# Strassen's scheme for eight more blocks of the first up projection and two more of the second, with the S5 setup batched over all groups

## The chip, the cores and the metric

The kernel runs on one core of a Trainium2 chip. The metric is the time of one execution in microseconds on the device; the time before is the median of three runs. One more execution was recorded by the hardware profiler.

## The reference

One decoder layer on a sequence of 512 tokens with 1024 channels, in float32:

```python
mod = (silu(c) @ w_ada + b_ada).reshape(9, 1024)      # sh1 sc1 g1 sh2 sc2 g2 sh3 sc3 g3
h = x * (1 + sc1) + sh1
x = layer_norm(ALPHA * x + 0.5 * g1 * ((silu(h @ w1) * (h @ w3)) @ w2))      # ffn1, 2816 wide
h = x * (1 + sc2) + sh2
x = layer_norm(ALPHA * x + g2 * hybrid_mixer(h))      # a Mamba-2 head group and an S5 head group
h = x * (1 + sc3) + sh3
x = layer_norm(ALPHA * x + 0.5 * g3 * ((silu(h @ w1) * (h @ w3)) @ w2))      # ffn2
```

The S5 group has 32 groups of 64 complex states. Before its scan can run, powers of the states' factors, and products of them with the input matrix B (called P) and the output matrix C (called Q), must be made from the parameters: this is the S5 setup.

## The kernel before

Every float32 matrix product is made of three matmuls: each operand is split into a high part (a rounded copy, made by ScalarE in `split`) and a low part (the rest, a subtraction on VectorE), and `mm3` adds high x high, high x low and low x high in PSUM (lines 101 to 105, so each product shows as L103, L104 and L105).

The up projections make 22 blocks f of 128 hidden channels, each with two matrices j (w1 and w3). In a plain block one such product has 8 steps of the inner dimension, 128x128 weights and 512 tokens: 24 matmuls of 512 columns. Of the second up projection the first two blocks are done in halves of the tokens, blocks 2 to 5 plainly, and blocks 6 to 21 (`FAST = 6`) in pairs by Strassen's scheme in `up_fast`: one unit is a pair of blocks and one j, a 2 x 2 arrangement of quarters (two halves of the inner dimension, two halves of the tokens, two blocks), with seven products (b11, t1, t2, b21, b22, t3, t4) of 4 steps with 256 columns, 84 matmuls. Sums of the weights (`wsum`, and sums written back into the raw tiles) are made for each unit by VectorE in `prep_a`, `prep_c`; sums of the activations once, by `h_sums`, into the three tiles `hs`, with a last one (`s4`) written over a quarter of the activations after the plain blocks.

Of the first up projection the first three blocks and half of the fourth run with the adaLN of h1 at the very start (to 60 us); the rest (`up`, line 1537) are plain blocks. Beside them run two lists of generators, advanced a fixed number of steps in each block: `jobs` holds the S5 setup (4 steps a block) and `ada`, from block 11 on, the remaining adaLN work (3 steps a block): loads of x, `ada_gate` for chunk 2 (g1), `ada_pair` for chunks 3 and 4 (m2), `ada_pair` for 6 and 7 (m3), `ada_gate` for chunk 5 (g2). One chunk is eight loads of 512 KB (tile `ra`, two buffers) each multiplied into one accumulator `acc` by VectorE (operations on L90), and then matmuls with ones (L295 for pairs, L318 and L319 for gates). What is left of `ada` is advanced once for each f of the first down projection (38 calls), and the rest is emptied behind it.

The S5 setup first computes parameters in 128x16 tiles, then runs four rounds b, each for four of the 16 pairs of groups: P, Q (128x64 operations), the matrices that are written to DRAM through the tile `s5mp` (two buffers, five uses a round), and the powers E (`Er`, `Ei`), which double their width seven times.

The down projections go over f in pairs, with `ghl` the split hidden activations, and end with a drain for each 128 tokens: the residual, the LayerNorm statistics, the normalisation and (first down) the transposed activations `hT` of the next stage.

The program is written in one order, and the framework's planner orders the instructions of each engine from it, so an instruction can stand earlier on its engine than it is written. Weights go over one queue, SP's, in a fixed order through four `raw` tiles; `wnext` splits two tiles ahead. `gate` rows have two buffers, and `wsum` takes one of them in the second up projection.

Of the kernel before, what the change touches and what calls it, by code (L numbers as in the profile page):

```python
# [10 lines left out]
F32 = mybir.dt.float32  # L11
# [8 lines left out]
P = 128  # L20
S = 512
# [29 lines left out]
class Layer:  # L51
    def __init__(self, tc, ctx, ins, out):
        self.tc, self.nc, self.ctx = tc, tc.nc, ctx
        self.i = ins
        self.out = out
        self.n = 0
        pool = lambda name, bufs, **k: ctx.enter_context(tc.tile_pool(name=name, bufs=bufs, **k))
        self.cp = pool("const", 1)
        self.ps = pool("ps", 8, space=PSUM)
        self.raw = pool("raw", 4)  # L60
        self.wsp = pool("wsp", 4)
        self.resp = pool("res", 1)
# [7 lines left out]
        self.pin = False  # L70

# [311 lines left out]

    def glue(self, gp, g, f, pa, pb):
        nc = self.nc
        if f % 2 == 0:
            self.gt = gp.tile([P, 2, S], F32, tag="g", bufs=NF // 2, name=self.nm("g"))
# [51 lines left out]
    def h_sums(self, hq, new, gp, gts):  # L439

        nc = self.nc
        v = lambda k, t: hq[k][:, 2 * t:2 * t + 2]
        hi, lo = lambda a: a[:, :, :, 0, :], lambda a: a[:, :, :, 1, :]
        for _ in range(3):
            gts.append(gp.tile([P, 2, S], F32, tag="g", bufs=NF // 2, name=self.nm("g")))
# [24 lines left out]
        join(y, v(1, 0))  # L472
        yield
        self.stt(y, y, -1.0, x, MUL, SUB)
        self.s4 = lambda: split(y, v(0, 1))

    def up_fast(self, hq, new, gp, gts, g, w, f0, last, jobs):
# [5 lines left out]
        v = lambda k, t: hq[k][:, 2 * t:2 * t + 2]  # L483
# [23 lines left out]
        c = self.gates.tile([P, 1024], F32, tag="gate", bufs=2, name="wsum")  # L507
# [45 lines left out]
        for u, (f, j) in enumerate(units):  # L553
            if j == 0:
                gt = gts.pop() if gts else gp.tile([P, 2, S], F32, tag="g", bufs=NF // 2, name=self.nm("g"))
                g.extend((gt[:, 0, :], gt[:, 1, :]))
            cp = self.tmp.tile([P, 4, 256], F32, tag="t4", name=self.nm("cp"))
# [19 lines left out]
            self.step(jobs, 1)  # L577
# [197 lines left out]
    def s5_setup(self, pre):  # L775
# [61 lines left out]
        E = (pt("Er", [P, 4, P]), pt("Ei", [P, 4, P]))  # L837
        w3 = [P, 4, 16]
        Pk = [(pt(f"p{k}r", w3), pt(f"p{k}i", w3)) for k in range(4)]
        Qk = [(pt(f"q{k}r", w3), pt(f"q{k}i", w3)) for k in range(4)]  # L840
        u1, u2 = pt("s5u1", w3), pt("s5u2", w3)
        mpart = lambda: pre.tile([P, 4, P], F32, tag="s5mp", bufs=2, name=self.nm("s5mp"))
        for b in range(4):
            q = slice(4 * b, 4 * b + 4)
            wb = lambda a: bc(a[:, q], (2, 16))
            dr = self.s5_dram[b]
            self.cmul(*Pk[0], wb(fr), wb(fi), bt['s5_b_re'][:, q], bt['s5_b_im'][:, q], u1, u2)
            for k in (1, 2, 3):
                if k == 2:
                    yield  # L850
                self.cmul(*Pk[k], wb(A[k][0]), wb(A[k][1]), *Pk[0], u1, u2)
            yield
            for n in range(2):
                for g in range(2):
                    sl = slice(64 * g, 64 * g + 64)
                    for k in range(4):
                        nc.scalar.copy(out=bd[n][sl, :, 3 - k, g, :], in_=Pk[k][n][sl])
                    nc.scalar.mul(out=cd[n][sl, :, g, :], in_=cb[('s5_c_re', 's5_c_im')[n]][sl, q, :],
                                  mul=(1.0, -1.0)[n])
            yield  # L860
            for j in range(4):
                if j == 2:
                    yield
                self.cmul(*Qk[j], wb(A[j + 1][0]), wb(A[j + 1][1]), cb['s5_c_re'][:, q],
                          cb['s5_c_im'][:, q], u1, u2)
# [9 lines left out]
            for n in range(2):  # L875
                M = mpart()
                nc.gpsimd.memset(M, 0.0)
                for g in range(2):
                    sl = slice(64 * g, 64 * g + 64)
                    for j in range(4):  # L880
                        nc.scalar.mul(out=M[sl].rearrange("p r (j g h) -> p r j g h", j=4, g=2)[:, :, j, g, :],
                                      in_=Qk[j][n][sl], mul=(1.0, -1.0)[n])
                nc.sync.dma_start(out=dr[:, 5 + n], in_=M)
                yield
            nc.vector.memset(E[0][:, :, 0:1], 1.0)
            nc.vector.memset(E[1][:, :, 0:1], 0.0)
            x1, x2 = [pre.tile([P, 4, 64], F32, tag="s5x", bufs=2, name=self.nm("s5x")) for _ in range(2)]
            for lg in range(7):
                n = 1 << lg
                er, ei = en[lg]  # L890
                self.cmul(E[0][:, :, n:2 * n], E[1][:, :, n:2 * n], bc(er[:, q], (2, n)), bc(ei[:, q], (2, n)),
                          E[0][:, :, 0:n], E[1][:, :, 0:n], x1[:, :, :n], x2[:, :, :n])
                if lg % 2 == 1:
                    yield
            for n in range(2):
                nc.sync.dma_start(out=dr[:, 2 + n], in_=E[n])
            yield
# [533 lines left out]
def body(tc, ins, out):  # L1431
# [3 lines left out]
    with ExitStack() as ctx:  # L1435
# [7 lines left out]
        L.want_up(ins['up1'], EARLY)  # L1443
        TAIL = 4
        HALVES = 2
        FAST = 6
# [12 lines left out]
        L.want_down(NF, ins['ffn1_w2'][0])  # L1459
        L.wlimit = len(L.wq)  # L1460
        L.want_mixer()
        L.want_up(ins['up2'], (), HALVES, g_alloc, FAST)
# [136 lines left out]
        gts = []  # L1599
        jobs = [L.h_sums(hx, hs, fp, gts), L.ada_gate(8, 0.5, g3)]  # L1600
        fast = L.up_fast(hx, hs, fp, gts, g, ins['up2'], FAST, down2, jobs)
        lead = [(next(fast) for _ in range(4))]
        L.up(hT3[0], fp, g, 0, jobs, 4, halves=HALVES, late=(lead, 4, FAST - 1), nf=FAST)
# [45 lines left out]
```

## Time and profile before

| | |
|---|---|
| median of three runs | 966.59 us (966.46 to 968.69) |
| profiled execution: its own time | 968.27 us |
| its span (first to last instruction) | 966.6 us |
| TensorE (PE) busy | 944.9 us, 98% |
| VectorE (DVE) busy | 758.4 us, 78% |
| ScalarE (ACT) busy | 446.9 us, 46% |
| GpSimd (POOL) busy | 34.2 us, 4% |
| mean granted TensorE clock | 0.995 |

The span is what the trace covers; 1.67 us of the profiled execution lie around it. Busy times are unions: an operation that starts before the last one has ended adds only what stands out. PE is the matmul row, PEld the weight loads beside it. The stages lie so: first up projection to 269.5 us, first down projection to 391, the mixer to 615, the second up projection to 838 (Strassen's units from 675), the second down projection to the end.

### The profile page before, as it was taken

How to read it: one execution, taken by the hardware profiler on the slowest of the kernel's cores; microseconds unless marked ns; L12 is line 12 of the kernel's file. 1: busy time of each engine (PE TensorE's matmuls, PEld its weight loads, DVE VectorE, ACT ScalarE, POOL GpSimd, SP SyncE). 2: the span in 40 equal slices, each digit the busy share in tenths (PEclk: the TensorE clock that was granted, in tenths of full speed). 3: DMA queues.
4: the chain of work that ended last, by engine and by line, in shares of the span. 5: the costliest groups of instructions: out<-in, count | busy, mean ns of one | idle time of the engine just before them, and what ended most of it. 6: DMA issues, size and time to landing. Idle time of an engine off the chain costs nothing.

```text
span 966.6 us, 14710 instructions
## 1 busy us (share of the span) xinstructions
PE 944.9 (98%) x5409; PEld 798.1 (83%) x5409; DVE 758.4 (78%) x1522; ACT 446.9 (46%) x879; POOL 34.2 (4%) x73
## 2 busy tenths in 40 slices
PE   8999999999999999999999999999999999999996
PEld 5778888887877888778877777988999999988885
DVE  6579998963677888858995889785788888896947
ACT  3343452635443335545537844533455554633420
POOL 0000000000000000100000110100000000000003
PEclk9999999999999999999999999999999999999999
DMA  9968584453866766362432024532233232543302
GB/s 342 377 190 270 188 280 162 157 174 122 261 204 197 242 217 180 86 233 71 142 121 67 1 88 152 173 111 66 88 99 120 89 129 90 175 152 109 109 1 87
DMA packets 75578, 147.93 MB, mean 153 GB/s; under 512 B 11633, under 2 KB 28657, under 8 KB 74993
## 3 DMA queue, kind: packets, MB, share of 16 engines
q1 hardware_dynamic: 75216, 146.94, 46.1%
q8 instruction: 42, 0.69, 0.3%
q14 instruction: 32, 0.25, 0.1%
q10 hardware_dynamic: 288, 0.04, 0.0%
HBM read 137.52 MB, written 9.44 MB: 152 GB/s over the span
## 4 chain that ended last, share of the span: by engine, by line
PE 86%; DVE 6%; ACT 4%; issue 2%; POOL 1%; DMA 0%; DVEq 0%; POOLq 0%; ACTq 0%
PE ps L103 27%; PE ps L104 27%; PE ps L105 27%; DVE cv L90 1%; PE ps L253 1%; PE ps L978 1%; DVE wlo L81 1%; PE ps L207 1%; ACT whi L96 1%; POOL rsx L170 1%; DVE s5X L81 0%; DMA raw<-in_w_in_dram 0%; PE ps L295 0%; DVE s5t L81 0%; PE ps L949 0%
## 5 line engine op out<-in xcount | busy, mean ns | idle before, releaser
L96 ACT CAST whi<-raw 128x1024 fp32r<-128x1024 f32 (+1 forms) x155 | 155.0, 1007 | 211.5 <-PE ps L104 97.5
L81 DVE TENSOR_TENSOR wlo<-raw,whi 128x1024 fp32r<-128x1024 f32 (+1 forms) x155 | 179.3, 1167 | 43.0 <-ACT whi L96 42.5
L103 PE MATMUL ps<-hT,whi 128*128 128x512 f32 x448 | 177.0, 396 | 1.7 <-ACT hT L1492 1.7
L104 PE MATMUL ps<-hT,whi 128*128 128x512 f32 x448 | 174.7, 390 | 0.1
L105 PE MATMUL ps<-hT,wlo 128*128 128x512 f32 x448 | 174.6, 390 | 0.0
L103 PE MATMUL ps<-whi,ghl 128*128 128x512 f32 x320 | 125.2, 391 | 0.0
L104 PE MATMUL ps<-wlo,ghl 128*128 128x512 f32 x320 | 124.5, 389 | 0.0
L105 PE MATMUL ps<-whi,ghl 128*128 128x512 f32 x320 | 124.3, 389 | 0.0
L103 PEld LDWEIGHTS ps<-hT,whi 128*128 128x128 f32 x448 | 83.9, 188 | 23.3 <-issue 3.2
L105 PEld LDWEIGHTS ps<-hT,wlo 128*128 128x128 f32 x448 | 84.1, 188 | 17.8
L104 PEld LDWEIGHTS ps<-hT,whi 128*128 128x128 f32 x448 | 84.2, 188 | 17.0 <-DVE hT L81 0.5
L103 PE MATMUL ps<-hx,whi 128*128 128x256 f32 (+1 forms) x320 | 97.5, 305 | 0.7 <-DVE cp L90 0.6
L104 PE MATMUL ps<-hx,whi 128*128 128x256 f32 (+1 forms) x320 | 97.3, 304 | 0.0
L105 PE MATMUL ps<-hx,wlo 128*128 128x256 f32 (+1 forms) x320 | 97.3, 304 | 0.0
L90 DVE SCALAR_TENSOR_TENSOR acc<-ra,cs,acc 128x1024 f32<-128x1024 f32 (+2 forms) x62 | 71.0, 1145 | 22.4 <-DMA ra<-in_w_ada_dram 21.9
L96 ACT CAST ghl<-g 128x512 fp32r<-128x512 f32 x88 | 53.1, 619 | 50.1 <-PE ps L105 37.5
L103 PEld LDWEIGHTS ps<-whi,ghl 128*128 128x128 f32 x320 | 60.1, 188 | 14.6 <-issue 2.5
L105 PEld LDWEIGHTS ps<-whi,ghl 128*128 128x128 f32 x320 | 60.1, 188 | 12.6
L104 PEld LDWEIGHTS ps<-wlo,ghl 128*128 128x128 f32 x320 | 60.1, 188 | 12.3
L81 DVE TENSOR_TENSOR ghl<-g,ghl 128x512 fp32r<-128x512 f32 x88 | 58.1, 686 | 13.6 <-ACT ghl L96 13.6
L103 PEld LDWEIGHTS ps<-hx,whi 128*128 128x128 f32 x320 | 61.1, 191 | 3.9 <-issue 0.8
L104 PEld LDWEIGHTS ps<-hx,whi 128*128 128x128 f32 x320 | 61.2, 191 | 2.6
(474 smaller groups left out, 1693.0 us busy)
## 6 DMA issues: line engine op xcount, KB each, us to landing
ra<-in_w_ada_dram SPq DMA_DIRECT2D x56, 512.0 KB, 4.5
raw<-in_up_dram SPq DMA_DIRECT2D x49, 512.0 KB, 4.2
raw<-in_ffn_w_dram SPq DMA_DIRECT2D x44, 512.0 KB, 4.4
raw<-in_up_dram SPq DMA_DIRECT2D x64, 256.0 KB, 3.8
ra<-in_ada_dram SPq DMA_DIRECT2D x16, 512.0 KB, 7.8
raw<-in_w_in_dram SPq DMA_DIRECT2D x16, 512.0 KB, 4.4
s5d<-s5mp SPq DMA_DIRECT2D x20, 256.0 KB, 3.8
s5M<-s5d SPq DMA_DIRECT2D x4, 1024.0 KB, 5.1
```

What stands on the lines that cost most here:

```text
L81: self.nc.vector.tensor_tensor(out=out, in0=a, in1=b, op=op)
L90: self.nc.vector.scalar_tensor_tensor(out=out, in0=a, scalar=s, in1=b, op0=op0, op1=op1, **k)
L96: keep(self.nc.scalar.copy(out=hi, in_=src))
L103: mm(o, lh, rh, start=first, stop=False, **k)
L104: mm(o, lh, rl, start=False, stop=False, **k)
L105: self.last_mm = mm(o, ll, rh, start=False, stop=last, **k)
L170: self.nc.gpsimd.tensor_scalar(out=x, in0=var, scalar1=EPS, scalar2=None, op0=ADD)
L207: self.nc.tensor.matmul(ps, self.onesr, bc(self.onesr, (1, 4)), start=True, stop=True)
L253: nc.tensor.matmul(bank[q:q + 32, 0:256], lhs, w[:, :, m * P:(m + 1) * P], start=(j < 2), stop=(j >= len(put) - 2))
L978: nc.tensor.matmul(pv[32 * r:32 * r + 32, j, :], M[:, n, r, 32 * j:32 * j + 32], rhs[:, r, :], start=(n == 0), stop=(n == 2))
```

## The change

Three things are changed. Blocks 14 to 21 of the first up projection (`FAST1 = 14`) go through `up_fast`, and `FAST` of the second falls from 6 to 4. `h_sums` and `up_fast` take the quarters as a function and the tile for the sums of weights from outside, and the copies `cp` come from a pool of their own. The S5 setup makes E in two halves of eight pairs of groups and P and Q for all 16 pairs at once, in five of the gate-activation tiles `g` that are not used yet (`spare`); the rounds b then only assemble and write the matrices. To fit, the setup has 6 steps a block instead of 4, and the adaLN list 2 steps in blocks 10 and 11, one in each unit, and one for each f of the first down projection as before; the down projection's weights are queued in the last unit (`down1`).

```diff
+    def g_tile(self, gp):
+        return self.spare.pop(0) if self.spare else gp.tile([P, 2, S], F32, tag="g", bufs=NF // 2, name=self.nm("g"))
...
-    def up_fast(self, hq, new, gp, gts, g, w, f0, last, jobs):
+    def up_fast(self, v, new, c, sp, gp, g, w, f0, last, jobs, per):
...
-        c = self.gates.tile([P, 1024], F32, tag="gate", bufs=2, name="wsum")
...
-            cp = self.tmp.tile([P, 4, 256], F32, tag="t4", name=self.nm("cp"))
+            cp = sp.tile([P, 3, 256], F32, tag="cp", bufs=2, name=self.nm("cp"))
...
-            self.step(jobs, 1)
+            self.step(jobs, per)
...
+        xt = big[4].rearrange("p a (q n) -> p a q n", n=64)
+        for h in range(2):
+            E = [big[2 * n + h].rearrange("p a (q t) -> p (a q) t", t=P) for n in range(2)]
+            q = slice(8 * h, 8 * h + 8)
+            nc.vector.memset(E[0][:, :, 0:1], 1.0)
+            nc.vector.memset(E[1][:, :, 0:1], 0.0)
+            for lg in range(7):
+                n = 1 << lg
+                er, ei = en[lg]
+                self.cmul(E[0][:, :, n:2 * n], E[1][:, :, n:2 * n], bc(er[:, q], (2, n)), bc(ei[:, q], (2, n)),
+                          E[0][:, :, 0:n], E[1][:, :, 0:n], xt[:, 0, :, :n], xt[:, 1, :, :n])
...
+        self.cmul(*Pk[0], wb(fr), wb(fi), bt['s5_b_re'], bt['s5_b_im'], u1, u2)
+        yield
+        for k in (1, 2, 3):
+            self.cmul(*Pk[k], wb(A[k][0]), wb(A[k][1]), *Pk[0], u1, u2)
+            yield
+        for j in range(4):
+            self.cmul(*Qk[j], wb(A[j + 1][0]), wb(A[j + 1][1]), cb['s5_c_re'], cb['s5_c_im'], u1, u2)
+            yield
...
-        FAST = 6
+        FAST1 = 14
+        FAST = 4
+        L.want_up(ins['up1'], EARLY, nf=FAST1)
...
+        wsum = [L.gates.tile([P, 1024], F32, tag="gate", bufs=2, name="wsum1")]
+
+        def down1():
+            L.want_down(NF, ins['ffn1_w2'][0])
+            L.wlimit = len(L.wq)
+            L.want_mixer()
+            L.want_up(ins['up2'], (), HALVES, g_alloc, FAST)
+            L.wahead(L.wi + 2)
...
-        jobs = [L.s5_setup(pre)]
+        L.spare = [L.g_tile(gp) for _ in range(NF // 2 - (len(g) + 1) // 2)]
+        jobs = [L.s5_setup(pre, L.spare[-5:])]
         ada = [xres(), L.ada_gate(2, 0.5, g1), L.ada_pair(3, m2), L.ada_pair(6, m3), L.ada_gate(5, 1.0, g2)]
-        L.up(hT, gp, g, f0, jobs, 4, late=(ada, 3, 11), done=pss[f0, 0])
+        L.up(hT, gp, g, f0, jobs, 6, late=(ada, 2, 10), done=pss[f0, 0], nf=FAST1 - 2)
         L.step(jobs, 1000)
         pctx.close()
+        sctx = ExitStack()
+        sp = sctx.enter_context(tile_pool("f1"))
+        hs = [sp.tile([P, 2, 4, 2, P], F32R, tag="hs", bufs=3, name=f"hs1{k}") for k in range(3)]
+        quarter = lambda k, t: hT[:, 2 * t:2 * t + 2, 4 * k:4 * k + 4]
+        jobs = [L.h_sums(quarter, hs, L.spare[-3:])]
+        fast = L.up_fast(quarter, hs, wsum[0], sp, gp, g, ins['up1'], FAST1, down1, ada, 1)
+        lead = [(next(fast) for _ in range(4))]
+        L.up(hT, gp, g, FAST1 - 2, jobs, 4, late=(lead, 4, FAST1 - 1), nf=FAST1)
+        L.step(jobs, 1000)
+        L.step(lead, 4)
+        next(fast)
+        ada.insert(0, fast)
+        sctx.close()
...
-        L.up(hT3[0], fp, g, 0, jobs, 4, halves=HALVES, late=(lead, 4, FAST - 1), nf=FAST)
+        L.up(hT3[0], fp, g, 0, jobs, 5, halves=HALVES, late=(lead, 4, FAST - 1), nf=FAST)
```

## Rows read from the trace of the kernel before

**Rows 1.** The page's first part: busy us, share of the span, instructions.

```profile
PE 944.9 (98%) x5409; PEld 798.1 (83%) x5409; DVE 758.4 (78%) x1522; ACT 446.9 (46%) x879; POOL 34.2 (4%) x73
```

**Rows 2.** Stages: us, busy PE, PEld, DVE, ACT, POOL, clock, DMA share, GB/s.

```profile
60.00:269.50 209.50, 209.50 (x991) 171.07 (x990) 167.01 (x656) 90.78 (x253) 6.33 (x12) 1.00 0.64 210
269.50:391.00 121.50, 121.50 (x539) 97.73 (x538) 98.08 (x126) 52.29 (x72) 0.79 (x2) 1.00 0.66 207
396.00:430.00 34.00, 32.12 (x146) 25.98 (x144) 23.77 (x35) 17.25 (x35) 2.10 (x7) 0.95 0.44 142
615.00:675.00 60.00, 60.00 (x333) 52.49 (x332) 44.26 (x48) 20.68 (x30) 0.00 (x0) 1.00 0.35 114
675.00:837.00 162.00, 161.32 (x1337) 160.40 (x1336) 132.30 (x195) 83.97 (x136) 0.00 (x0) 1.00 0.32 105
```

**Rows 3.** Timeline of PE around 675 us: start, us, engine, line, operation.

```profile
671.91 0.39 PE L105 MATMUL ps<-hx,wlo 128*128 128x512 f32 x1
...
674.63 0.39 PE L105 MATMUL ps<-hx,wlo 128*128 128x512 f32 x1
...
675.45 0.28 PE L105 MATMUL ps<-hx,wlo 128*128 128x256 f32 x1
...
677.37 0.28 PE L103 MATMUL ps<-hs,whi 128*128 128x256 f32 x1
```

**Rows 4.** Timeline of VectorE in the first up projection, operations behind one another.

```profile
56.65 1.22 DVE L81 TENSOR_TENSOR wlo<-raw,whi 128x1024 fp32r<-128x1024 f32 x1 [0.25 <-ACT whi L96]
57.79 0.68 DVE L81 TENSOR_TENSOR g<-sl,ps 128x512 f32<-128x512 f32 x1
58.39 1.22 DVE L81 TENSOR_TENSOR wlo<-raw,whi 128x1024 fp32r<-128x1024 f32 x1
...
150.34 0.42 DVE L81 TENSOR_TENSOR s5x<-e6i,Ei 128x256 f32<-128x256 f32 x1
150.68 0.22 DVE L81 TENSOR_TENSOR s5u<-a1r,p0r 128x64 f32<-128x64 f32 x1
150.81 0.42 DVE L81 TENSOR_TENSOR Er<-s5x,s5x 128x256 f32<-128x256 f32 x1
```

**Rows 5.** Groups by line, 60 to 240 us: busy us, mean ns, idle before.

```profile
L90 DVE SCALAR_TENSOR_TENSOR acc<-ra,cs,acc 128x1024 f32<-128x1024 f32 x14 | 17.9, 1281 | 0.7 <-DMA ra<-in_w_ada_dram 0.7
...
L81 DVE TENSOR_TENSOR s5x<-e6r,Er 128x256 f32<-128x256 f32 x4 | 1.7, 422 | 0.1
...
L81 DVE TENSOR_TENSOR s5u<-a1r,s_c_re 128x64 f32<-128x64 f32 x4 | 0.9, 226 | 0.0
```

**Rows 6.** The chain that ended last: start, us, engine, what.

```profile
240.35 0.98 PE ps L295 x4
...
337.95 0.98 PE ps L295 x4
...
375.53 0.50 DVE gate L90
```

**Rows 7.** DMA issues: count, KB each, median us to landing.

```profile
ra<-in_w_ada_dram SPq DMA_DIRECT2D x56, 512.0 KB, 4.5
```

**Rows 8.** PE at the mixer's entry (timeline), and its one wait 676 to 840.

```profile
399.39 0.62 PE L105 MATMUL ps<-zw,hT 128*128 128x512 f32 x1 [1.14 <-DVE hT L81]
...
402.36 0.63 PE L103 MATMUL ps<-zw,hT 128*128 128x512 f32 x1
...
PE ps L103 <- DVE cp L90: 0.6, 1, 0.6
```

**Rows 9.** Timeline of the last S5 round: two tiles copied, buffers taken again.

```profile
237.20 1.07 ACT L872 COPY s5mp<-ps 128x512 f32<-128x512 f32 x2 [2.33 <-PE ps L870]
...
240.63 0.52 POOL L877 MEMSET s5mp<- 128x512 f32 x1 [30.94 <-DMA s5d<-s5mp]
...
244.91 0.53 POOL L911 MEMSET s5mp<- 128x512 f32 x1 [3.04 <-DMA s5d<-s5mp]
```

**Rows 10.** Busy time in 57.4 to 145 us, columns as in rows 2.

```profile
57.40:145.00 87.60, 87.60 (x404) 72.18 (x404) 85.67 (x409) 38.41 (x97) 1.58 (x3) 1.00 0.77 254
```

More of the change, by code (lines that the diff above doesn't have):

```diff
@@ L70, in __init__ @@
         self.pin = False
+        self.spare = []
     def nm(self, s):
@@ L386, in glue @@
         if f % 2 == 0:
-            self.gt = gp.tile([P, 2, S], F32, tag="g", bufs=NF // 2, name=self.nm("g"))
+            self.gt = self.g_tile(gp)
         s = self.tmp.tile([P, 512], F32, tag="t2", name=self.nm("sl"))
@@ L436, in up, with h_sums @@
                 pss.append(ps)
-    def h_sums(self, hq, new, gp, gts):
+    def h_sums(self, v, new, gts):
         nc = self.nc
-        v = lambda k, t: hq[k][:, 2 * t:2 * t + 2]
         hi, lo = lambda a: a[:, :, :, 0, :], lambda a: a[:, :, :, 1, :]
-        for _ in range(3):
-            gts.append(gp.tile([P, 2, S], F32, tag="g", bufs=NF // 2, name=self.nm("g")))
         x, y, z = [t.rearrange("p a (b q) -> p (a b) q", q=P).rearrange("p (t k) q -> p t k q", t=2)
@@ L554, in up_fast @@
             if j == 0:
-                gt = gts.pop() if gts else gp.tile([P, 2, S], F32, tag="g", bufs=NF // 2, name=self.nm("g"))
+                gt = self.g_tile(gp)
                 g.extend((gt[:, 0, :], gt[:, 1, :]))
-            cp = self.tmp.tile([P, 4, 256], F32, tag="t4", name=self.nm("cp"))
+            cp = sp.tile([P, 3, 256], F32, tag="cp", bufs=2, name=self.nm("cp"))
             p1, u2, p5 = [cp[:, n] for n in range(3)]
@@ L772, in cmul, with s5_setup @@
             self.tt(o, t, t2, op)
-    def s5_setup(self, pre):
+    def s5_setup(self, pre, big):
         nc, i = self.nc, self.i
@@ L836, in s5_setup @@
             nc.gpsimd.memset(t, 0.0)
[L837 to L841, printed above, removed]
+        xt = big[4].rearrange("p a (q n) -> p a q n", n=64)
[9 more added lines that the diff above has]
+                          E[0][:, :, 0:n], E[1][:, :, 0:n], xt[:, 0, :, :n], xt[:, 1, :, :n])
+                if lg in (3, 5):
+                    yield
+            for b in range(2):
+                for n in range(2):
+                    nc.sync.dma_start(out=self.s5_dram[2 * h + b][:, 2 + n], in_=E[n][:, 4 * b:4 * b + 4])
+            yield
+        v4 = lambda t: t.rearrange("p a (c q h) -> p (a c) q h", c=2, h=16)
+        PQ = [v4(t) for t in big[:4]]
+        Pk = [(PQ[k // 2][:, 2 * (k % 2)], PQ[k // 2][:, 2 * (k % 2) + 1]) for k in range(4)]
+        Qk = [(PQ[2 + k // 2][:, 2 * (k % 2)], PQ[2 + k // 2][:, 2 * (k % 2) + 1]) for k in range(4)]
+        u = v4(big[4])
+        u1, u2 = u[:, 0], u[:, 1]
+        wb = lambda a: bc(a, (2, 16))
+        self.cmul(*Pk[0], wb(fr), wb(fi), bt['s5_b_re'], bt['s5_b_im'], u1, u2)
+        yield
+        for k in (1, 2, 3):
+            self.cmul(*Pk[k], wb(A[k][0]), wb(A[k][1]), *Pk[0], u1, u2)
+            yield
+        for j in range(4):
+            self.cmul(*Qk[j], wb(A[j + 1][0]), wb(A[j + 1][1]), cb['s5_c_re'], cb['s5_c_im'], u1, u2)
+            yield
         mpart = lambda: pre.tile([P, 4, P], F32, tag="s5mp", bufs=2, name=self.nm("s5mp"))
@@ L844, in s5_setup @@
             q = slice(4 * b, 4 * b + 4)
-            wb = lambda a: bc(a[:, q], (2, 16))
             dr = self.s5_dram[b]
[L847 to L852, printed above, removed]
             for n in range(2):
@@ L856, in s5_setup @@
                     for k in range(4):
-                        nc.scalar.copy(out=bd[n][sl, :, 3 - k, g, :], in_=Pk[k][n][sl])
+                        nc.scalar.copy(out=bd[n][sl, :, 3 - k, g, :], in_=Pk[k][n][sl, q])
                     nc.scalar.mul(out=cd[n][sl, :, g, :], in_=cb[('s5_c_re', 's5_c_im')[n]][sl, q, :],
                                   mul=(1.0, -1.0)[n])
[L860 to L865, printed above, removed]
             yield
@@ L881, in s5_setup @@
                         nc.scalar.mul(out=M[sl].rearrange("p r (j g h) -> p r j g h", j=4, g=2)[:, :, j, g, :],
-                                      in_=Qk[j][n][sl], mul=(1.0, -1.0)[n])
+                                      in_=Qk[j][n][sl, q], mul=(1.0, -1.0)[n])
                 nc.sync.dma_start(out=dr[:, 5 + n], in_=M)
                 yield
[L885 to L897, printed above, removed]
             ps = self.bank([P, P])
@@ L1442, in body @@
         L.early = len(L.wq)
-        L.want_up(ins['up1'], EARLY)
         TAIL = 4
         HALVES = 2
-        FAST = 6
+        FAST1 = 14
+        FAST = 4
+        L.want_up(ins['up1'], EARLY, nf=FAST1)
         def g_alloc():
@@ L1458, in body @@
         g1, g2, g3, m2, m3 = [], [], [], [], []
[L1459 to L1462, printed above, removed]
+        wsum = [L.gates.tile([P, 1024], F32, tag="gate", bufs=2, name="wsum1")]
[5 more added lines that the diff above has]
+            L.wahead(L.wi + 2)
         hctx, gctx, pctx, fctx, xctx = [ExitStack() for _ in range(5)]
@@ L1598, in down2, with sums @@
             L.wahead(L.wi + 2)
-        gts = []
-        jobs = [L.h_sums(hx, hs, fp, gts), L.ada_gate(8, 0.5, g3)]
-        fast = L.up_fast(hx, hs, fp, gts, g, ins['up2'], FAST, down2, jobs)
+        wsum2 = L.gates.tile([P, 1024], F32, tag="gate", bufs=2, name="wsum2")
+        quarter = lambda k, t: hx[k][:, 2 * t:2 * t + 2]
+        def sums():
+            own = [L.g_tile(fp) for _ in range(3)]
+            yield from L.h_sums(quarter, hs, own)
+            L.spare = own
+        jobs = [sums(), L.ada_gate(8, 0.5, g3)]
+        fast = L.up_fast(quarter, hs, wsum2, sp, fp, g, ins['up2'], FAST, down2, jobs, 1)
         lead = [(next(fast) for _ in range(4))]
-        L.up(hT3[0], fp, g, 0, jobs, 4, halves=HALVES, late=(lead, 4, FAST - 1), nf=FAST)
+        L.up(hT3[0], fp, g, 0, jobs, 5, halves=HALVES, late=(lead, 4, FAST - 1), nf=FAST)
         L.step(lead, 4)
```

1 line of the change is left out of this document (removed).

## The prediction

> **What bounds the kernel now.** I read the page's first part, then busy time by stage, then PE's waits. The page shall show one thing: TensorE is busy 98% of the span, the next engine, VectorE, 78% [rows 1]. By stage the picture is sharper. In the rest of the first up projection (60 to 269.5 us) and in the first down projection PE is busy for every microsecond, although VectorE has 167.0 of 209.5 and 98.1 of 121.5 us of work beside it [rows 2]. The second up projection's Strassen blocks (675 to 837) lose 0.68 of 162 us. Only the entry of the mixer has a hole: 1.88 us in 396 to 430 [rows 2]. So time falls only where PE gets fewer columns, and only as long as VectorE, ScalarE and the DMA queues stay ahead of it.
>
> **What the change takes from PE.** In a plain block matmuls of 512 columns start 2.72 us apart per twelve, 0.2267 each; in a Strassen block those of 256 columns start 1.92 us apart per sixteen, 0.120 each [rows 3]. A pair of f blocks costs 2 x 2 x 8 x 3 = 96 of the first, 21.76 us; as two units of seven products it costs 2 x 7 x 4 x 3 = 168 of the second, 20.16 us. One pair saves 1.60 us, not the eighth (2.72) that the count of columns promises, because a half-size matmul does not take half the time. The busy time of weight loads says why: 160.4 of 162 us with the half-size matmuls against 171.1 of 209.5 with the full ones [rows 2]. Four pairs of the first up projection and one more of the second: 5 x 1.60 = 8.0 us.
>
> [...]
>
> **What the change puts on VectorE.** A Strassen unit occupies VectorE for 132.3 / 16 = 8.27 us [rows 2], so eight take 66.2 us. They replace 16 low parts and 8 products with the silu; by start-to-start times (1.14 us for 128x1024, 0.60 for 128x512 [rows 4]) 23 us. Net +43. The sums of activations (h_sums and its last split) are twelve operations of 128x1024 and one more: 14.8 us, new in the first up projection.
>
> The batched S5 setup gives some of it back. Per round of four pairs of groups the trace has 48 operations of 128x64 for P and Q; behind one another these start 0.13 us apart, and 128x256 ones 0.34 apart [rows 4]. 4 x 48 x 0.13 = 25 becomes 48 x 0.34 = 16. The powers E are 42 operations a round, growing from 4 to 256 columns: some 6.4 us each round by the same pitches, 25 in all; in two halves of twice the width some 19. About 15 us saved, of some 84 that the setup holds now (167.0 less 42 for low parts, 11 for products, 30 for adaLN).
>
> [...]
>
> So the first up projection holds 167 + 43 + 15 - 15 = 210 us of VectorE work in about 203. It fits only because adaLN moves out.
>
> **What moves.** The adaLN jobs are 70 steps (4 loads of x; gate 2: 11; pair 3: 22; pair 6: 22; gate 5: 11). Before, 33 were called in the up and the other 37 in the down's 38 calls, and the last gate lands just at its end (375.53 [rows 6]). After it is 4 + 8 in the up and 38 in the down: 50. The last 20 steps (five accumulations of chunk 7, its matmuls and transposes, all of gate 5) come behind the down projection in the program. They carry 13 loads of 512 KB on SP (4.5 us to landing [rows 7]) ahead of the mixer's rows and weights, and 13 accumulations of 1.28 us [rows 5] on VectorE, where the residual drains, the hT split and the LayerNorm rows queue behind them. The work is not free to go earlier: one accumulator serves all, and each chunk waits for PE to consume the last (four such steps, 240.35 to 337.95 [rows 6]); chunk 6's matmuls now come at the 35th of 38 calls, so chunk 7 can begin only some 25 us before the end, and chunk 5 after it. That leaves 8 x 1.2 + 1.1 + 1.2 = 12 us for the entry of the mixer. There VectorE is idle for 34 - 23.8 = 10.2 us [rows 2], and PE waits 1.14 us for hT [rows 8].
>
> [...] Bounds: nothing if the steps fill idle time, 5.1 us if each of the four drains meets one accumulation of 1.28. I take 1.5, nearer to nothing because the drains have priority.
>
> **The entry of the Strassen stage.** The first fast product is now due at 269.6 - 87 (blocks 14 to 21) - 1 to 2 of matmuls that belong to later jobs, near 181. Before that the setup must be through: its tiles are the spare gate tiles that h_sums takes, and hs lies on its pool. VectorE has until then 21 low parts (24), 11 products (6.6), the setup (84 - 15 = 69), h_sums (14.8) and the first unit's preparation (4): 118 of 121 us. Then the chain: a round of the setup sends five tiles through two buffers, whose turns are 3.4 and 4.3 us (237.20 to 240.63 to 244.91 [rows 9]), some 6 for the fifth; 10.7 a round, 43 for four. P is through after 29.5 (parameters: 84 less 25 + 25 for P, Q, E and 4.5 for the diagonals) + 19 (E) + 8 (P) = 56.5 us of VectorE work, at the 73% that low parts and products leave (1.14 x 2 + 0.60 in 10.88): 60 + 77 = 137; the rounds end at 180. Just in time. Each accumulation drawn forward before it delays all of this (gate 2's eight: 9 us). Bounds 0 and 14.2 (rival c); I take 1.5, near the low end because VectorE ran 98% full through the same stretch today without one wait of PE [rows 2, 10].
>
> The stage itself: today's sixteen units cost PE 0.68, of which one wait of 0.6 at the join to the down projection [rows 8]; the new join gets the same, +0.6. cp leaves the tile tag it shared with the gate splits, which excludes a wait and adds none. wsum takes one of two gate rows, so gate 5's bias row is loaded only after the last unit, hidden behind 120 us of down projection. In the second up h_sums and gate 8 lose two plain blocks: 44.3 us of VectorE work in 615 to 675, less 6 for the blocks, in 43.5 us; +0.2.
>
> **Sum.** -8.0 + 1.5 + 1.5 + 0.6 + 0.2 = -4.2. The profiled execution took 968.27 us (span 966.6 and 1.67 around it) and would take 964.1. The runs' median is 966.59, 1.7 lower; from it 962.4, rounded to **962**. I call 0.3% (2.9 us) what can be told from no change, so faster is below 963.7, slower above 969.5.
>
> **Rivals.** (a) Everything hides: -8.0 + 0.6 - 0.6, **958.6**. For it: PE never waited in the up and down projections. Chance 0.20. (b) The entry of the mixer pays in full: 5.1 + 1.7 in place of 1.5 makes 967.7, half of it 964.3; call it **966**. For it: the leftover 12 us exceed 10.2 of idle time. Chance 0.17. (c) The other side: the setup is late. With gate 2's accumulations drawn forward P is through at 60 + (56.5 + 9)/0.73 = 150, the rounds at 193; the first split of h_sums (a copy and a subtraction of 128x1024, 2.2) then lets t1 start at 195 instead of 182.4 (181 and the first product): PE idles 12.5, and 1.7 at the lower clock follows. 966.6 - 8.0 + 14.2 + 1.5 + 0.8 = **975**. It decides from about 7 us of delay. Against it: S5 steps stand ahead of adaLN in the program. Chance 0.13. (d) VectorE becomes the bound inside the fast units: 66.2 + eight adaLN steps (9.6) + gate 2's split and sums (2.3) = 78.1 of 80.6. If the 29.7 us of idle in 162 today [rows 2] cannot be used, 14.8 come on top, and the stage is 12.3 longer: **974**. Chance 0.08.
>
> **Chances.** The forecast (959.5 to 963.7) 0.42, (a) 0.20, (b) 0.17, (c) 0.13, (d) 0.08. Faster 0.62, same 0.17, slower 0.21. The likeliest case alone reaches from 959.5 to 963.7; the range for 8 in 10 runs from 957.8 (all hidden and the mixer's hole a little smaller) to 970, which leaves most of (c) and (d) out.
>
> **What the profile after would show.** The first down starts 5 to 7 us earlier; blocks 14 to 21 run at 0.120 per matmul; VectorE at 95% or more up to there. A wait of PE for hs or for whi near 181 means (c). Accumulations between the drains and a longer hole before the z matmuls mean (b). PE waits spread over the units, released by wlo, mean (d). The prediction is wrong if PE idles above 5 us in all more than today, or if half-size matmuls take other than 0.120 in the first up projection.

## The result, and the profile after

The changed kernel takes 1036.39 us (median of four runs, 1035.09 to 1038.28) where the kernel before takes 967.37 (966.46 to 968.69) on the same chip: a ratio of 1.0711, 95% interval 1.0696 to 1.0725. It is slower by 69 us; the forecast was 4.2 us faster.

The page's first part says at once that PE got no more to do: it is busy as long as in [rows 1] (944.9 us), in a span that is 70 us longer. VectorE has 54 us more to do, ScalarE 32, but in the longer span their shares are 78% and 46%, as before. The list of PE's waits, below it, says where it stands (line, what released it: us in all, times, longest). Lines of the changed kernel are one higher in the helpers and 14 to 20 higher in the S5 setup than those of before.

```profile
PE 945.1 (91%) x5769; PEld 813.7 (79%) x5769; DVE 812.6 (78%) x1397; ACT 479.3 (46%) x938; POOL 35.2 (3%) x73
```

```profile
PE ps L884 <- ACT bd L877: 42.4, 4, 36.3
PE ps L319 <- ACT gs L97: 22.9, 1, 22.9
```

Busy time by stage, columns as in [rows 2], puts the two waits in their places:

```profile
60.00:118.60 58.60, 58.60 (x259) 48.25 (x257) 55.06 (x253) 16.08 (x23) 0.00 (x0) 1.00 0.79 258
118.60:155.00 36.40, 0.10 (x2) 0.09 (x2) 33.42 (x84) 4.30 (x15) 0.00 (x0) 0.56 0.44 153
155.00:231.00 76.00, 68.89 (x350) 54.80 (x351) 42.91 (x71) 53.27 (x196) 6.31 (x12) 0.92 0.38 125
231.00:311.30 80.30, 79.70 (x665) 79.52 (x664) 67.87 (x98) 43.89 (x71) 0.00 (x0) 1.00 0.34 115
...
420.00:480.00 60.00, 32.60 (x139) 24.71 (x138) 42.28 (x59) 18.39 (x33) 4.84 (x10) 0.74 0.56 167
...
745.00:907.00 162.00, 161.39 (x1341) 161.05 (x1341) 136.60 (x202) 84.43 (x137) 0.00 (x0) 1.00 0.32 105
```

Between 118.6 and 155 PE does nothing, in the middle of the plain blocks. The Strassen stage itself (231 to 311.3) and the second up projection (745 to 907) are as full as those of before. The first down projection starts at 311.30 where it started at 269.59, 41.7 later; the mixer's first z matmul, 397.51 before, comes at 467.89, 70.4 later. So 41.7 us are lost in the first up projection, 28.7 in the down projection and the entry of the mixer. Behind that the mixer loses 1.2 and the second up projection gives 1.45 back.

The first hole on the timelines (start, us, engine, what, and in brackets the idle time before it and what ended it), of VectorE, ScalarE, SP and PE in turn:

```profile
100.34 0.17 DVE L82 TENSOR_TENSOR g<-e0r,g 128x8 f32<-128x8 f32 x1
...
124.71 1.28 DVE L91 SCALAR_TENSOR_TENSOR acc<-ra,cs,acc 128x1024 f32<-128x1024 f32 x1
...
145.52 0.42 DVE L82 TENSOR_TENSOR g<-s5fr,s_b_re 128x256 f32<-128x256 f32 x1
```

```profile
146.78 0.50 ACT L877 COPY bd<-g 64x64 f32<-64x64 f32 x2 [27.28 <-DVE g L82]
```

```profile
130.69 15.62 SPq L852 DMA_DIRECT2D s5d<-g  x8
```

```profile
154.94 1.09 PE L884 MATMUL ps<-ident,bd 128*128 128x128 f32 x4 [36.30 <-ACT bd L877]
...
167.94 1.03 PE L884 MATMUL ps<-ident,bd 128*128 128x128 f32 x8
```

VectorE begins E at 100.34 and P at 145.52; in between stand E's operations and, drawn forward by the planner, the accumulations of adaLN chunk 3 (the last at 124.71). ScalarE stands at the copies of P into `bd` for 27.28 us, and behind it wait the casts of the next weights; SP stands at E's DMAs for 15.6 us, and behind them wait the loads (none is issued between 128.76 and 171.15). PE has come to the first round's transposes at 118.6 and stands there: matmuls of the next plain block are behind them in its order. In the kernel before, P's first product (VectorE) stands at 83.09, ahead of E, and the first round's transposes (PE) run at 115.71 without a wait:

```profile
83.09 0.22 DVE L81 TENSOR_TENSOR s5u<-s5fr,s_b_re 128x64 f32<-128x64 f32 x1
...
115.71 1.03 PE L870 MATMUL ps<-ident,bd 128*128 128x128 f32 x8
```

The second hole, on PE and on VectorE:

```profile
439.68 1.05 PE L296 MATMUL ps<-acc,ones 128*32 128x512 f32 x4
...
465.62 1.22 PE L319 MATMUL ps<-gs,onesr 128*128 128x512 f32 x2 [22.87 <-ACT gs L97]
```

```profile
441.45 0.74 DVE L86 TENSOR_SCALAR acc<-ra,cs 128x1024 f32<-128x1024 f32 x1
...
457.72 1.28 DVE L91 SCALAR_TENSOR_TENSOR acc<-ra,cs,acc 128x1024 f32<-128x1024 f32 x1 [1.69 <-DMA ra<-in_w_ada_dram]
...
468.91 1.22 DVE L82 TENSOR_TENSOR zw<-raw,zw 128x1024 fp32r<-128x1024 f32 x1
```

Chunk 5 can begin only when PE has taken chunk 7 (439.68). Its eight accumulations last from 441.45 to 464.4, at the pace of the loads (VectorE idles 1.4 to 1.7 us before each of the last five), and the split of the mixer's weights, `zw`, stands behind them on VectorE as PE's z matmuls stand behind L319.

### The profile page after: what moved, and what is told of

The parts are those of the page before. It is cut to its first block, busy times and chain, and to the rows that moved or that the text cites. A ratio compares the mean times of both kernels' runs of the same rounds, so it can differ in the third digit from the quotient of the medians.

```text
span 1036.6 us, 15442 instructions
## 1 busy us (share of the span) xinstructions
PE 945.1 (91%) x5769; PEld 813.7 (79%) x5769; DVE 812.6 (78%) x1397; ACT 479.3 (46%) x938; POOL 35.2 (3%) x73
## 4 chain that ended last, share of the span: by engine, by line
PE 72%; DVE 14%; DMA 5%; ACT 4%; issue 3%; POOL 1%; SPq 0%; DVEq 0%; POOLq 0%; ACTq 0%
PE ps L105 22%; PE ps L104 22%; PE ps L106 22%; DMA ra<-in_w_ada_dram 4%; DVE g L82 3%; DVE acc L91 2%; DVE wlo L82 2%; DMA s5d<-s5mp 1%; DVE cv L91 1%; PE ps L254 1%; DVE s5t L82 1%; PE ps L979 1%; PE ps L208 1%; ACT s5mp L916 1%; ACT whi L97 1%
## 5 line engine op out<-in xcount | busy, mean ns | idle before, releaser
L97 ACT CAST whi<-raw 128x1024 fp32r<-128x1024 f32 (+1 forms) x165 | 160.6, 982 | 201.4 <-PE ps L106 70.8
L82 DVE TENSOR_TENSOR wlo<-raw,whi 128x1024 fp32r<-128x1024 f32 (+1 forms) x165 | 185.7, 1139 | 53.9 <-ACT whi L97 53.6
L104 PE MATMUL ps<-hT,whi 128*128 128x512 f32 (+1 forms) x448 | 164.7, 369 | 2.3 <-ACT hT L1498 1.7
L105 PE MATMUL ps<-hT,whi 128*128 128x512 f32 (+1 forms) x448 | 162.9, 364 | 0.1
L106 PE MATMUL ps<-hT,wlo 128*128 128x512 f32 (+1 forms) x448 | 162.4, 363 | 0.0
L104 PE MATMUL ps<-whi,ghl 128*128 128x512 f32 x320 | 125.1, 391 | 0.0
L105 PE MATMUL ps<-wlo,ghl 128*128 128x512 f32 x320 | 124.6, 389 | 0.0
L104 PEld LDWEIGHTS ps<-hT,whi 128*128 128x128 f32 x448 | 85.6, 192 | 18.4 <-issue 3.8
L105 PEld LDWEIGHTS ps<-hT,whi 128*128 128x128 f32 x448 | 85.7, 191 | 12.5 <-DVE hT L82 0.5
L104 PE MATMUL ps<-hx,whi 128*128 128x256 f32 (+1 forms) x320 | 94.0, 294 | 0.6 <-DVE cp L91 0.6
L105 PE MATMUL ps<-hx,whi 128*128 128x256 f32 (+1 forms) x320 | 94.0, 294 | 0.0
L106 PE MATMUL ps<-hx,wlo 128*128 128x256 f32 (+1 forms) x320 | 93.9, 294 | 0.0
L104 PE MATMUL ps<-hs,whi 128*128 128x256 f32 x312 | 88.3, 283 | 0.0
L105 PE MATMUL ps<-hs,whi 128*128 128x256 f32 x312 | 88.3, 283 | 0.0
L106 PE MATMUL ps<-hs,wlo 128*128 128x256 f32 x312 | 88.3, 283 | 0.0
L104 PEld LDWEIGHTS ps<-whi,ghl 128*128 128x128 f32 x320 | 60.1, 188 | 14.8 <-ACT ghl L97 2.5
L105 PEld LDWEIGHTS ps<-wlo,ghl 128*128 128x128 f32 x320 | 60.1, 188 | 12.2
```

Source lines behind the costliest of these rows:

```text
L82: self.nc.vector.tensor_tensor(out=out, in0=a, in1=b, op=op)
L97: keep(self.nc.scalar.copy(out=hi, in_=src))
L104: mm(o, lh, rh, start=first, stop=False, **k)
L105: mm(o, lh, rl, start=False, stop=False, **k)
L106: self.last_mm = mm(o, ll, rh, start=False, stop=last, **k)
```

## The experiments

Edits are against the kernel changed, where nothing else is said. A single time is one execution.

**The adaLN list emptied inside the down projection.**

```diff
-        L.down(NF, ..., 6, ada, 1)
+        L.down(NF, ..., 6, ada, 2)
```

> The changed kernel with one number altered: the list of adaLN steps is advanced twice, not once, for each f of the first down projection, so it is through before that projection ends. Theory: the 20 steps left over behind the down projection, paced by their loads, make the hole ahead of the mixer's z matmuls; it should go, the wait of PE at L319 (22.9 us) with it, and the time fall by 24 to 29 us, to 1007 to 1012. The hole of 36 us in the first up projection stays. Rival 1: the same accumulations now make VectorE the bound of the down projection (98 us of its work in 121.5 before, 17 more now), the hole only moves into it, and less than 12 us are won. Rival 2: the hole comes from the loads of the mixer's weights alone and nothing is won.

Measured: 1024.5, a gain of 12, half of the least that the theory said. The wait at L319 fell to 1.1, but PE now stood in the down projection (10.2 us at L296); the place was right, the free room was not. This is what rival 1 said would come, but not by VectorE's sum: VectorE idled 8.8 us for loads among these accumulations. The longest of the waits, 7.8 us, is one of order: VectorE makes the drains of the down projection's first half (373.93 to 381.1) ahead of the accumulation that PE waits for.

**P and Q ahead of E.**

```diff
-        for h in range(2):
-            E = [big[2 * n + h]...]      # then P, Q
+        # P, Q first
+        E = [pt(f"E{n}", [P, 8, P]) for n in range(2)]
+        for h in range(2):
```

> The changed kernel with P and Q made ahead of the powers E; E gets tiles of its own, as it can no longer share theirs. Theory: PE stands 36.3 us at the transposes of the first S5 round because P comes behind 45 us of E on VectorE; with P first, it is there when PE arrives near 118, this wait falls below 5 us, the first down projection starts at 270 to 276 where it started at 311.3, and the time falls by 34 to 42 us, to 994 to 1002. Rival 1: VectorE has too much work ahead of the fast blocks in any order; PE then waits later, for hs or wlo near 181, and less than 20 us are won. Rival 2: the four DMAs of E stand in SP's queue ahead of the weights and PE waits for whi instead.

Measured: 1003.41, a gain of 33, 1 us short of what was expected. The 36.3 us are gone, the first down projection starts at 275.96. So the order of E and P was this hole's cause; rivals 1 and 2 fall, though small waits stay in the rounds:

```profile
PE ps L319 <- ACT gs L97: 21.0, 1, 21.0
PE ps L909 <- ACT k L906: 5.1, 3, 2.6
PE ps L884 <- ACT bd L877: 4.1, 2, 2.3
```

**Both.**

> Both edits together: P and Q ahead of E, and two adaLN steps for each f of the first down projection. Theory: the two holes are independent and their prices add, so the time is 960 to 970, and the 8 us of PE columns come out as a gain over the kernel before. Rival: VectorE is the bound in the first up or the first down projection once both holes are gone; the time stays above 972.

Measured: 994.55, ratio 1.0283 (1.0265 to 1.0301); the theory missed by 25 us. The waits at L296, 11.2 us in all, show a good part of why; another 7.3 stayed at the rounds (L909, L884). PE, then VectorE:

```profile
295.61 1.05 PE L296 MATMUL ps<-acc,ones 128*32 128x512 f32 x4
317.32 1.05 PE L296 MATMUL ps<-acc,ones 128*32 128x512 f32 x4 [1.39 <-DVE acc L91]
348.74 1.92 PE L296 MATMUL ps<-acc,ones 128*32 128x512 f32 x4 [7.89 <-DVE acc L91]
```

```profile
143.81 1.28 DVE L91 SCALAR_TENSOR_TENSOR acc<-ra,cs,acc 128x1024 f32<-128x1024 f32 x1 [0.18 <-DMA ra<-in_w_ada_dram]
...
296.98 0.75 DVE L86 TENSOR_SCALAR acc<-ra,cs 128x1024 f32<-128x1024 f32 x1
...
340.24 1.28 DVE L82 TENSOR_TENSOR dr<-ps,gate 128x512 f32<-128x512 f32 x2
...
347.41 1.27 DVE L91 SCALAR_TENSOR_TENSOR acc<-ra,cs,acc 128x1024 f32<-128x1024 f32 x1
```

Chunk 3's sum is complete at 145, but PE's matmuls that read it are called in the down projection, at 295.6. For 150 us the one accumulator is held and no chunk can begin; then four are crowded into the down projection, 21.7 to 31.4 us from one chunk's matmuls to the next where the doubled steps leave some 15. The longest wait, 7.9 us, has the drains in it again: they stand on VectorE from 340.24 to 347.4, ahead of the last accumulation that PE waits for.

**Most of adaLN left out.**

> The changed kernel with six of the eight loads and accumulations of each later adaLN chunk left out (chunks 2 to 8 are wrong by that); the steps, matmuls and everything else stay. It measures what the accumulations drawn forward cost the S5 setup. Theory: 12 of the 16 accumulations that VectorE made between 79 and 126 us are gone, 14 to 17 us with their waits for loads, and the wait of 36.3 at the first round's transposes falls to 17 to 24; the hole ahead of the mixer goes too; 990 to 998. Rival 1: the order of E and P alone makes that wait, which stays above 30. Rival 2: the accumulations make it, and it falls below 8.

Measured: 1001.84, some 4 us more than expected; 5.3 us of waiting remained ahead of the mixer. The wait at the first transposes is 19.7, within the theory's range: leaving out twelve of the sixteen accumulations takes 16.6 of the 36.3 us away. The two causes overlap and are no shares of one sum: with P first and all sixteen kept, the wait goes as well, because P, through near 105, then stands ahead of chunk 3's eight.

**The adaLN steps taken in the Strassen units.** P first, and four steps in each unit in place of one.

> P and Q ahead of E (as in the second run), and the adaLN list advanced four times, not once, in each Strassen unit of the first up projection; one step for each f of the first down projection, as in the kernel changed. Theory: in the two runs with two steps for each f PE waits 10 us at L296 because there is one accumulator: chunk 3's sums are ready near 155, but PE's matmuls that free the accumulator stand in the program behind 270, so three more chunks, some 21 us each through two load buffers, are crowded into the down projection. With 32 steps in the units PE takes chunks 3 and 4 there, 34 steps are left for 38 calls, and neither L296 nor L319 waits more than 3 us: 970 to 980 in place of 1003.4. Rival: VectorE is the bound in the units (8 to 9 us more of accumulations in 80): waits of PE on wlo or cp there of 6 us or more, and 982 to 990.

Measured: 980.25, at the upper end of what was expected. L296 and L319 are no longer among the waits of 1 us or more: the held accumulator was the second hole. What remained is 8.2 us at the rounds (L909, L884) and 4.2 of idling at the join to the down projection (270 to 300).

**E woven into the rounds.**

> The run before, and E no longer stands between Q and the rounds of the S5 setup: its six steps are taken inside the rounds, and PE's transposes of k4 stand one more step behind its copy. In the two runs with P first PE waits 4.7 us there and 2 to 4 at the rounds' first transposes, and the clock falls to 0.91 to 0.95 in 118 to 155. Theory: the rounds begin one block earlier and stand further apart, the waits go, and the time is 5 to 12 us under the run before it. Rival: P is not ready a block earlier (it was through at 105) or the rounds' copies, not their places, set the pace; then 0 to 3 us.

Measured: 982.0, ratio 1.0138 (1.0119 to 1.0157): the rival. The waits only moved, from L909 to L105 (`hs`, 2.6) and L104 (`cp`, 3.3) in 180 to 210, and those at the rounds' first transposes grew from 2.8 to 5.4.

**The batch alone.**

> The batched S5 setup alone: all 22 blocks of the first up projection are plain, adaLN runs at three steps a block from block 11 as before, and Strassen's scheme in the second up projection starts at block 6 as before. Theory: the hole at the first round's transposes comes from E standing ahead of P at VectorE, not from the Strassen units, so PE waits there 25 to 37 us and the time is 992 to 1005, although there is 15 us less work for VectorE. Rival: the hole needs the tight schedule of the whole change (six steps a block and adaLN from block 10 are the cause); then the batch alone costs under 5 us. Here six steps a block are kept.

Measured: 1009.91, above the 992 to 1005 expected, with the same wait in a first up projection without any Strassen unit. The batch at six steps a block, meant to relieve VectorE, cost 42 of the 69 us. Only half of the rival is answered by that: adaLN ran from block 11, but with the four steps a block of before PE would come to the transposes later, and this was not run.

```profile
PE ps L884 <- ACT bd L877: 39.9, 3, 36.1
```

**Strassen's scheme with the old setup.**

> Strassen's scheme as in the kernel changed, but with the S5 setup of before, round by round, at eight steps a block to be through in time, and four adaLN steps in each unit. Theory: P of the first round comes ahead of its E, so the hole of 36 us goes, but VectorE has some 15 us more to do ahead of the first fast product, 133 in 121, so PE is held up there by 5 to 20 us: 970 to 985. Rival: the old setup finds its time, and the time is below 966, so the batch was never needed.

Measured: 1000.99, worse than the theory by 16. At eight steps a block PE reaches the first transposes at 91, before P again (9.9 us), and in the program each later round's P stands behind the E of the round before; PE waits there six times, 25.7 us in all. With the same steps in the units, the batch with P first (980.25, at six steps a block) is 21 us faster: of the two setups tried, the batch in another order is the one that serves the change.

**Fewer pairs.** In these two runs and in the later ones with three pairs P is first, E woven in, and one of the five tiles moves into the setup's own pool.

```diff
-        FAST1 = 14
+        FAST1 = 16
-        L.up(hT, gp, g, f0, jobs, 6, late=(ada, 2, 10), ...)
+        L.up(hT, gp, g, f0, jobs, 5, late=(ada, 3, 11), ...)
```

> Strassen's scheme in the first up projection from block 16 on (three pairs in place of four), P and Q ahead of E with E's steps inside the rounds, five S5 steps a block, adaLN at three steps a block from block 11 (as before) and four in each unit. Theory: what is left of the loss (waits at the rounds, at hs and at the units' first products, 982.0 in all) is VectorE having 118 us of work or more in 121 us ahead of the first fast product; one pair fewer moves that product 10.9 us back and takes 10.8 us of work off the first up projection, at 1.6 us of PE columns: the waits shrink to 2 to 6 us, and the time is 962 to 967. Rival: the waits at the rounds come from the chain of copies through two s5mp buffers at ScalarE, whatever VectorE has to do; then 970 to 976.

> The same with two pairs (from block 18 on) and four S5 steps a block, as before. Theory: with still more room all waits that the change brought are gone, three pairs of columns remain (two here, one in the second up projection), 4.8 us: 963 to 966. Rival of the run before: the rounds' chain now has its old distance, so its waits go here and not there; then this run is below the run with three pairs by 4 us or more.

Measured: three pairs 972.16 (ratio 1.0046, 1.0029 to 1.0062), not in the theory's range but in the rival's; two pairs 978.1 (1.0100, 1.0079 to 1.0121). The second tells nothing of the question: with two pairs only two tiles are left where `h_sums` takes three, a plain block's product overwrites one of its sums (so the units' activations are wrong there), and PE waits 5.9 us for `hT`.

**The second up projection alone**, in the kernel before; then with tiles of its own for `cp`. The jobs beside its plain blocks take five steps a block in both, not four.

```diff
-        FAST = 6
+        FAST = 4
...
-            cp = self.tmp.tile([P, 4, 256], F32, tag="t4", name=self.nm("cp"))
+            cp = sp.tile([P, 3, 256], F32, tag="cp", bufs=2, name=self.nm("cp"))
```

> The kernel before with Strassen's scheme in the second up projection from block 4, not 6, and nothing else. By the columns 1.6 us less, with 0.2 for a fuller VectorE 1.4: a ratio of 0.9985 (0.9978 to 0.9995). Rival: h_sums comes too late ahead of the units, one pair earlier, and PE waits there; then no change or a loss of up to 2 us.

> The kernel before with Strassen's scheme in the second up projection from block 4, as run alone before (971.1, a loss of 3.6, with a wait of 2.0 for whi at 718 beside a split of the gate's sums and a clock of 0.91 behind it), but the copies cp get tiles of their own, as the kernel changed has them, and no longer share two tiles with the gate's split. Theory: the loss came from that sharing; now the columns show: 964.5 to 966.5, a ratio of 0.997 to 0.999. Rival: the gate's accumulations in the units make it, wherever cp lies; then 969 to 971 again.

Measured: with the shared tiles 971.07, ratio 1.0029 (1.0018 to 1.0039); with tiles of its own 966.69, 0.9987 (0.9976 to 0.9999). The loss, larger than even the rival allowed, lay in the sharing. In the first, `PE ps L103 <- ACT whi L96: 2.0, 1, 2.0` stands beside the last half of the gate's split; by which step the sharing delays this cast was not traced.

**Three `s5mp` buffers, adaLN from block 9.** For room, `k4` and the diagonals of C lie in the tiles of B, which P has read by then.

> The run with three pairs (fast from block 16), with three s5mp buffers in place of two, adaLN from block 9 on at three steps a block and three, not four, in each unit. In that run PE still waited 4.3 us at the rounds (with the clock at 0.95 in 118 to 155) and 4.0 at the join to the down projection, where VectorE did three accumulations between the parts of the last unit. Theory: the first comes from the two buffers that the rounds' tiles go through, the second from the accumulations crowded into the last units; both go, 4.3 + 1.9 + 4.0 + 1.8 = 12 us at most, 8 expected: 962 to 967 (972.2 before). Rival: the order of the instructions at ScalarE, not the buffers, makes the rounds late; then 966 to 970.

> All four pairs (fast from block 14), P and Q ahead of E, with three s5mp buffers, adaLN from block 9 on at three steps a block and three in each unit. Without the last two 980.3. Theory: VectorE has 118 us of work in 121 ahead of the first fast product, and any wait in the rounds comes through; the buffers give 3 to 6 us, the join 3: 970 to 976, still above the kernel before. Rival: the loss left was all buffers and the join; then 960 to 966, and the four pairs pay after all.

Measured: three pairs 968.03, ratio 1.0008 (0.9998 to 1.0019), 4.1 us won where 8 were expected, which is in the rival's range; four pairs 977.31, 1.0098 (1.0081 to 1.0114), 1 us above what was expected. With three pairs 118 to 155 is full (PE busy 37.00 of 37 us) and PE keeps its clock there (1.00); with four it still waits 9.0 us for the k4 copies, in 118 to 180. So the third buffer and the moved adaLN steps together won part of the loss (which of them was not run), but they do not save the fourth pair. I had put that down to VectorE's sum ahead of the first fast product. VectorE's busy time from 60 us to that product does not tell the two apart: it is 125.2 of 133.8 us with four and 138.2 of 146.6 with three, 94% in both. The two runs also differ in E's place, in the distance of k4's transposes from its copy and in the steps a block (the first two changed together, with two buffers, gave nothing above). Why the fourth pair does not pay stays open. What was left with three pairs stands at the last unit:

```profile
268.40 0.36 PE L104 MATMUL ps<-hT,whi 128*128 128x256 f32 x1 [1.47 <-DVE cp L91]
272.46 1.05 PE L296 MATMUL ps<-acc,ones 128*32 128x512 f32 x4 [2.40 <-DVE acc L91]
```

**Fewer steps in the units**, against the run with three pairs and three buffers.

```diff
-        late=(ada, 3, 9)      # and 3 in each unit
+        late=(ada, 4, 9)      # and 2 in each unit
```

> The run with three pairs and three s5mp buffers, with four adaLN steps a block from block 9 on and two, not three, in each unit. There PE still lost 3.9 us in 210 to 300, for cp and for chunk 4's accumulator at the last unit, and 2.7 at one round. Theory: with fewer steps in the units the accumulations stand further from the last unit and 2 to 4 us are won: 964 to 966, the first version under both kernels with the Strassen units in the first up projection. Rival: chunk 4 then falls into the start of the down projection and PE waits there instead: no change, 967 to 969.

Measured: 965.2 (963.06 to 966.0), ratio 0.9967 (0.9955 to 0.9978): faster than both kernels, by 3.2 us where its four pairs take 6.4 from PE. Busy time around the rounds, the units and the join (columns as above):

```profile
118.00:155.00 37.00, 36.22 (x194) 28.99 (x193) 34.28 (x81) 27.90 (x106) 2.57 (x5) 1.00 0.82 271
155.00:180.00 25.00, 23.50 (x134) 18.43 (x133) 22.75 (x59) 17.70 (x73) 3.10 (x6) 1.00 0.72 248
...
210.00:270.00 60.00, 59.15 (x480) 56.83 (x479) 51.43 (x73) 30.61 (x50) 0.00 (x0) 1.00 0.53 172
270.00:300.00 30.00, 28.65 (x130) 23.47 (x129) 27.32 (x37) 13.67 (x21) 0.00 (x0) 1.00 0.82 279
```

PE still idles 4.5 us in these 152, where before it idled nowhere, and VectorE is at 91 to 93% outside the units.

## Why the prediction was wrong, step by step

**What the change takes from PE: right.** The units run from 229.84 to 311.30, 81.5 us; 672 matmuls at 0.120 and the join's 0.6 make 81.2. The second up projection takes 230.95 us where it took 232.40: 1.45 less, close to the 1.6 of its one pair. Rival (d), a bound within the units, did not come: PE is busy 79.7 of 80.3 us there. Of the two signs that the prediction gave for being wrong, half-size matmuls other than 0.120 did not come; PE idling above 5 us more than today did.

**The entry of the Strassen stage: the step that failed.** "60 + 77 = 137; the rounds end at 180. Just in time": I dated P and the rounds against the first fast product near 181. But PE does not first meet the setup there. It meets it at the first round's transposes, which six steps a block place in block 8, at 118.6. By my own date P was 18.4 us late for them; with most accumulations left out the chip showed 19.7. I had taken it that plain blocks would go on meanwhile. They could not: PE, ScalarE (copies of P ahead of the weights' casts) and SP (E's DMAs ahead of the weights' loads) each stood at what came first in their order. In the 36.3 us not one matmul of the next block runs, in the 27.28 us at its copy ScalarE makes no cast, and in the 15.62 us of E's DMAs SP issues no load.

Two sizes beside it were off. I allowed gate 2's eight accumulations to be drawn forward, against which "S5 steps stand ahead of adaLN in the program"; sixteen accumulations came, and leaving out twelve of them takes 16.6 us off the wait. [rows 5] could have said so: it counts fourteen such operations in the kernel before. And E and P ran slower than their pitch where nothing lay between (E's second half 12.8 us in place of 9.5, below; P's first six operations 2.51, 145.52 to 148.03, in place of 6 x 0.34 = 2.04). The rounds, put at 43 us in all, last 63 here, from 154.94 to the last write of their tiles at 218.18 (what paces them was not traced). Rival (c) named the late setup, but at the wrong place and at 12.5 us; the batch alone cost 42. The 1.7 us for a lower clock that rivals (b) and (c) add no run shows; it is an estimate, 0.05 x 34, from the mixer's entry in [rows 2]. What the changed kernel showed is a clock of 0.50 and 0.93 in the two stretches of 5 us behind this wait, 2.9 us (an estimate, below), and of 0.50 and 0.52 in 465.6 to 470 and 470 to 475, behind the 22.87 us at the entry.

**What moves: the place right, the size wrong.** I saw that chunk 7 could begin 25 us before the end of the down projection and chunk 5 only after it, and then priced the rest by VectorE's time, 12 us that idle time takes up: +1.5. A chunk is not 8 x 1.28 of VectorE but some 22 us of loads through two buffers, behind a single accumulator whose reader stands in PE's order. The entry paid 28.7 with the down projection, four times rival (b). The two runs with doubled steps and the one with the steps in the units show the chain: crowding the steps moves the wait to L296, taking chunk 3 early removes it.

**The second up projection: right in this kernel**, for a reason that I had costed at nothing: "cp leaves the tile tag it shared with the gate splits, which excludes a wait and adds none". Without that edit the same two blocks lose 3.6 us.

**The sum of VectorE's work** (118 of 121 us) left out the accumulations drawn forward. In the run with four pairs and three buffers VectorE is busy 125.2 us ahead of the first fast product, which comes at 193.79 and not near 181; sixteen accumulations, some 19 us, are in that, so the rest was nearer 106 (an estimate). With them the stretch was over its room. Whether this is what keeps four pairs 10 us behind once both holes are mended is not shown; with three pairs part of the gain shows.

## What to carry to other kernels

Date each operand against the place where its first reader stands in that engine's order, not against the stage that needs the last result; and when a setup is batched, make first what the waiting engine asks for first (here P, for which PE stood 36.3 us). Count a chain by what paces it (loads through its buffers, one accumulator, the place of the matmul that frees it), not by the busy time of the engine that does the arithmetic. Where a sum leaves the second engine 97% full, try a smaller share of the change as well: here three pairs won 3.2 us and the best run with four lost 10, though the cause of that difference was not singled out.

## What the runs showed of the hardware

In E's second half VectorE's operations that read the result of the one just before started later than those that did not. With nothing between, two products of 128x256 start 0.34 apart, but the sum that reads both starts 0.45 behind the second, and the next product, written over what the sum has read, another 0.46:

```profile
138.91 0.42 DVE L82 TENSOR_TENSOR g<-e5r,g 128x256 f32<-128x256 f32 x1
139.25 0.42 DVE L82 TENSOR_TENSOR g<-e5i,g 128x256 f32<-128x256 f32 x1
139.70 0.42 DVE L82 TENSOR_TENSOR g<-g 128x256 f32<-128x256 f32 x1
140.16 0.43 DVE L82 TENSOR_TENSOR g<-e5r,g 128x256 f32<-128x256 f32 x1
```

So this half took 12.8 us (132.76 to 145.52) where the pitch of [rows 4] gave 9.5; that pitch, 0.34, lies between two operations that do not depend on one another, and in the kernel before such other work stood between (the one at 150.68 there). The batch lengthens the operations but also takes away what lay between them.

After its 36.3 us of idling PE came back slower: the four transposes at 154.94 took 1.09 us where eight take 1.03 at 167.94. The granted clock (last column but two) is 0.50 behind that idling, 0.93 in 160 to 165 and 1.00 in 165 to 170; it falls again, to 0.83, in 180 to 200, where PE idles 3.6 us:

```profile
155.00:160.00 5.00, 4.83 (x15) 3.85 (x16) 4.73 (x13) 2.28 (x8) 0.53 (x1) 0.50 0.28 105
...
180.00:200.00 20.00, 16.38 (x78) 12.61 (x77) 4.68 (x8) 15.30 (x68) 2.63 (x5) 0.83 0.46 151
```

From 155 to 231 it is 0.92, some 6 us (0.08 x 76) on top of the waits: by these rows 2.9 us behind the 36.3 (0.50 x 5 and 0.07 x 5) and 3.4 in 180 to 200 (0.17 x 20), estimates both.
